# One fused VectorE operation for the second conditioning row of the modulation sums

## The chip, the cores and the metric

The kernel runs on one core of a Trainium2 chip. The metric is the device time of one execution in microseconds. The engines are named as in the profile: PE (TensorE, the matmuls), DVE (VectorE), ACT (ScalarE), POOL (GpSimd) and SP (SyncE, which here only issues DMAs). Each engine works through its own list of instructions in order; an instruction that waits holds up everything behind it on its engine.

## The reference, cut to what matters

The program is one block of a diffusion-style model followed by two transformer layers with experts. The change lies in the first block. Its modulation vectors are a matrix product of two conditioning rows, `c` for the 256 tokens of `x` and `c_ctx` for the 256 tokens of `ctx`, and its first feed-forward runs over all 512 tokens:

```python
mod   = (silu(c)     @ w_ada + b_ada)      # 9 * 1024 values, for x
mod_c = (silu(c_ctx) @ w_ada + b_ada)      # the same for ctx
h  = rmsnorm(x, g0) * (1 + mod[1]) + mod[0]
x  = x + 0.5 * mod[2] * rmsnorm((silu(h @ w_gate) * (h @ w_up)) @ w_out, g)
# ctx likewise with mod_c[0..2]; then both are modulated with entries 3 and 4
```

Entries 0 and 1 are needed before the feed-forward starts. Entries 2 to 4 are needed for both rows, entries 5 to 8 for `x` alone, and none of them before the feed-forward's end.

## The kernel before, in words

Entries 0 and 1 (2,048 of the 9,216 columns of `w_ada`) are computed by matmuls. The other 7,168 are cut into 56 tiles of 128 features. A tile of `w_mod` has its 128 features on the partitions and the 1,024 inputs along the row, so one value of `mod` is the sum along a row of weight times silu of a conditioning row. `crow[0]` and `crow[1]` hold these two rows, repeated on all partitions (their buffers show as `xn` in the profile, as does the scratch output `mscr`). `mod_tiles(n)` handles the next n tiles. Tiles 16 to 39 in its counting need both rows (`rs = 2`), tiles 40 to 71 one. For row 0 a DVE `scalar_tensor_tensor` (L600) multiplies and sums in one instruction, with a short accumulator read behind it. For row 1 POOL multiplies in place (L597) and ACT copies the product in place with a sum along the row (L598). When eight tiles are done, POOL adds the bias (L603).

These tiles are handled between the matmuls of the feed-forward. Its 22 hidden units of 128 features, j = 0 to 21, each take two weight tiles (gate and up), each 24 matmuls of 128x512: every fp32 product is taken as three products of a high and a low part (L154, L155, L156). `Weights._prepare` makes these parts from a loaded tile `raw`: ACT writes the high part (L100, `split..h`), DVE subtracts (L101, `split..l`). Only a few pairs of parts are kept ahead. After a unit's matmuls, ACT takes the silu (L502, `gate`), DVE multiplies (L504, `hid`), and the product is split again (ACT L150, DVE L151). After unit 10 the first half of the output product follows (`swiglu_out`), with tiles of `w_mod` between its steps, then units 11 to 21 and the second half.

The first 18 tiles of `w_mod` come through a ring of four buffers of their own (`own`), the rest through the six buffers of the weights' ring. All loads are issued by SP in one list (L83), each as soon as the last reader of its buffer is done. The order on each engine is set by the framework's scheduler when the kernel is built, not by the order of the code.

Of the kernel before, what the change touches and what calls it, by code (L numbers as in the profile page):

```python
# [13 lines left out]
AF = mybir.ActivationFunctionType  # L14
OP = mybir.AluOpType
# [109 lines left out]
def build(tc, A, out):  # L125
    nc = tc.nc
    es = ExitStack()
    V, SC, PE, GP = nc.vector, nc.scalar, nc.tensor, nc.gpsimd
# [29 lines left out]
    def rsqrt(pool, v, n):  # L158
        t = pool.tile([128, n], I32, name="rs_t", bufs=2)
        y = pool.tile([128, n], FT, name="rs_y", bufs=4)  # L160
        w = pool.tile([128, n], FT, name="rs_w", bufs=2)
        V.tensor_scalar(t, v.bitcast(I32), 1, None, op0=OP.logical_shift_right)
        V.tensor_scalar(y.bitcast(I32), t, -1.0, float(0x5F3759DF), op0=OP.mult, op1=OP.add)
        for _ in range(3):
            V.scalar_tensor_tensor(w, y, -0.5, v, op0=OP.mult, op1=OP.mult)
            V.tensor_tensor(out=w, in0=w, in1=y, op=OP.mult)
            V.scalar_tensor_tensor(y, w, 1.5, y, op0=OP.add, op1=OP.mult)  # L167
        return y
# [408 lines left out]
    crow, mscr = {}, None  # L577
# [4 lines left out]
    mscr = pf.tile([128, D], FT, name="xn", bufs=4)  # L582
# [5 lines left out]
    def mod_tiles(n):  # L588
        for _ in range(n):
            f = next(late)  # L590
            rs = 2 if f < 40 else 1
            src = own if f < 34 else st
            w = src.take(held)
            for r in range(rs):
                m = mod[:, f, r:r + 1]
                if r:
                    GP.tensor_tensor(out=w, in0=w, in1=crow[r], op=OP.mult)  # L597
                    SC.activation(w, w, AF.Copy, accum_out=m)  # L598
                else:
                    V.scalar_tensor_tensor(mscr, w, 1.0, crow[r], op0=OP.mult, op1=OP.mult, accum_out=m)  # L600
            if f % 8 == 7:
                m = mod[:, f - 7:f + 1, 0:rs]
                GP.tensor_tensor(out=m, in0=m, in1=cols[:, OB + f - 7:OB + f + 1, None].to_broadcast([128, 8, rs]), op=OP.add)  # L603
            src.more(held)

    st.slots("split", pf, 1, "in8", tag="hid2", bufs=12)
    for j in range(2, FT_N):
        hs.append(swiglu_in(pf, hT, 512, 12))
        mod_tiles(mod_in(j))
        if j == 10:  # L610
            Y = [pf.tile([128, D], FT, name="y1", tag="Y", bufs=4) for _ in range(4)]
            for h, t, P in swiglu_out(hs, range(4), after=lambda u: mod_tiles(mod_out(u))):
                (copy_act if t % 2 else V.tensor_copy)(Y[t][:, 512 * h:512 * h + 512], P)
            hs = []
            st.slots("split", pf, 1, "in19", tag="hid2", bufs=12)
# [11 lines left out]
    for r in range(2):  # L627
        ts = range(2 * r, 2 * r + 2)
        G = gate_rows(pf, 0, r, 0.5)
        posts = {t: Post(pf, tok[t], G, Y[t]) for t in ts}  # L630
        for h, t, P in swiglu_out(hs, ts, after=first_rows if r else (lambda u: mod_tiles(mod_last(u)))):
            posts[t].half(h, P)
        late_posts = [posts[t] for t in ts]
        if r:
            for p in late_posts:
                p.finish()
# [303 lines left out]
    for i in range(2):  # L940
        a, w = attention(i), within(i)
# [216 lines left out]
    for l in range(2):  # L1158
# [50 lines left out]
        r = rsqrt(pa, css.rearrange("p a b -> p (a b)"), 4)  # L1209
# [96 lines left out]
        for i in range(2):  # L1306
# [5 lines left out]
            for g0 in range(4):  # L1312
# [17 lines left out]
                for j in range(n // 2):  # L1330
# [3 lines left out]
                                           op0=OP.mult, op1=OP.add)  # L1334
# [14 lines left out]
            r = rsqrt(pa, ss, 4)  # L1349
# [38 lines left out]
        for p in range(2):  # L1388
            for i in range(2):
                for b in blocks(i):  # L1390
                    for s in range(2):
# [14 lines left out]
                        in1=rt[64:96, 1, None, :256].to_broadcast([32, 4, 256]), op=OP.add)  # L1406
# [107 lines left out]
        for d in range(DT):  # L1514
# [18 lines left out]
            m = pg.tile([128, 256], FT, name="msum", bufs=2)  # L1533
# [496 lines left out]
```

## Time and profile before

| | |
|---|---|
| median of three runs | 2044.76 us (2040.51 to 2051.39) |
| profiled execution, its own time | 2043.18 us |
| span in the profile | 2041.4 us |
| mean granted TensorE clock | 0.960 |
| PE busy | 1832.6 us (90%) |
| DVE busy | 1085.5 us (53%) |
| ACT busy | 785.5 us (38%) |
| POOL busy | 238.6 us (12%) |

The time outside the span is 1.8 us. Busy times are sums over the whole span, and an instruction that is held up after it has started counts as busy. The granted clock is 1 at 2.4 GHz and 0.5 at 1.2 GHz. The feed-forward's units with both rows and the first half of its output product lie between 60 and 215 us of the span.

### The profile page before, as it was taken

The numbers are of one execution on the slowest core, as the hardware profiler recorded it, in microseconds if no ns is written. First come the engines' busy times: TensorE is split into PE (matmuls) and PEld (weight loads), VectorE is DVE, ScalarE is ACT, GpSimd is POOL, SyncE is SP. The second block draws the span as 40 slices with busy tenths as digits, with TensorE's granted clock in tenths as the row PEclk, the third lists the DMA queues.
The fourth block names the chain that finished last, engine by engine and source line by source line (L and its number), as shares of the span: only waits on it lengthen the run. The fifth ranks groups of instructions, "written<-read, shape, count | busy, mean of one in ns | idle before, by whom it ended". The sixth has DMA issues, their size and how long they took to land. (4 is left out here: it accounts for less than half of the span.)

```text
span 2041.4 us, 29593 instructions
## 1 busy us (share of the span) xinstructions
PE 1832.6 (90%) x11486; PEld 1415.3 (69%) x11486; DVE 1085.5 (53%) x2086; ACT 785.5 (38%) x1369; POOL 238.6 (12%) x170
## 2 busy tenths in 40 slices
PE   6979999999989997999998998877879999979686
PEld 2768788877777797998888997424238889853331
DVE  4774465484646667555678556311257864641113
ACT  4443232353534445444455543211135465331111
POOL 2552100031122211000100011000010000200000
PEclk9989999999999998999998999998989899989798
DMA  8533475343131154555433478998963336899897
GB/s 322 190 141 122 170 254 208 132 155 106 65 117 63 63 169 135 188 188 190 148 125 103 135 268 311 360 412 345 413 263 135 105 124 204 309 357 413 352 413 282
DMA packets 120120, 436.63 MB, mean 214 GB/s; under 512 B 13616, under 2 KB 13664, under 8 KB 119968
## 3 DMA queue, kind: packets, MB, share of 16 engines
q1 hardware_dynamic: 116208, 422.63, 56.4%
q0 software_dynamic: 2608, 8.32, 1.2%
q10 hardware_dynamic: 1152, 3.67, 0.5%
q8 instruction: 94, 1.54, 0.3%
q14 instruction: 58, 0.48, 0.1%
HBM read 433.51 MB, written 1.05 MB: 213 GB/s over the span
## 5 line engine op out<-in xcount | busy, mean ns | idle before, releaser
L101 DVE TENSOR_TENSOR split7l<-raw,split7h 128x1024 fp32r<-128x1024 f32 x98 | 123.9, 1264 | 113.2 <-ACT split7h L100 112.9
L1697 PE MATMUL ax<-raw,xg 128*32 128x512 f32 x1024 | 166.1, 596 | 7.0 <-DMA raw<-in_moe 7.0
L101 DVE TENSOR_TENSOR split6l<-raw,split6h 128x1024 fp32r<-128x1024 f32 x99 | 127.4, 1286 | 84.5 <-ACT split6h L100 82.9
L100 ACT ACTIVATE split7h<-raw 128x1024 fp32r<-128x1024 f32 x101 | 106.7, 1057 | 166.6 <-PE mm L156 63.3
L100 ACT ACTIVATE split6h<-raw 128x1024 fp32r<-128x1024 f32 x102 | 107.9, 1058 | 153.8 <-PE mm L155 46.8
L1697 PEld LDWEIGHTS ax<-raw,xg 128*32 128x32 f32 x1024 | 37.2, 109 | 107.2 <-issue 59.6
L1668 PE MATMUL ax<-OH,X 128*128 128x128 f32 x512 | 71.8, 301 | 38.0 <-DVE OH L1659 35.9
L1668 PEld LDWEIGHTS ax<-OH,X 128*128 128x128 f32 x512 | 67.6, 213 | 54.7 <-DVE OH L1659 36.8
L600 DVE SCALAR_TENSOR_TENSOR xn<-raw,xn 128x1024 f32<-128x1024 f32 x56 | 85.0, 1517 | 22.0 <-DMA raw<-in_w_mod 21.2
L1724 PE MATMUL ax<-raw,ehT 128*32 128x512 f32 x512 | 77.1, 607 | 16.6 <-ACT ehT L147 15.6
L597 POOL TENSOR_TENSOR raw<-raw,xn 128x1024 f32<-128x1024 f32 x24 | 72.5, 3034 | 76.6 <-DVE xn L600 73.0
L1731 DVE SCALAR_TENSOR_TENSOR yl<-ax,gsl,yh 128x512 fp32r<-128x512 f32 x32 | 24.0, 751 | 99.0 <-ACT yh L1730 94.6
L377 ACT ACTIVATE xg<-ax,cols 128x128 f32<-128x128 f32 x64 | 24.1, 458 | 94.4 <-PE ax L1668 68.6
L1705 ACT ACTIVATE ehs<-ax 128x256 f32<-128x256 f32 x16 | 6.2, 384 | 137.7 <-PE ax L1697 137.7
L1706 DVE TENSOR_TENSOR ehs<-ax,ehs 128x256 f32<-128x256 f32 x16 | 6.8, 425 | 97.7 <-ACT ehs L1705 97.7
L1724 PEld LDWEIGHTS ax<-raw,ehT 128*32 128x32 f32 x512 | 17.6, 109 | 59.1 <-issue 27.8
L154 PE MATMUL mm<-hThi,split6h 128*128 128x512 f32 x128 | 53.1, 415 | 5.5 <-ACT split6h L100 3.5
L156 PE MATMUL mm<-hThi,split6l 128*128 128x512 f32 x128 | 53.0, 414 | 4.8 <-DVE split6l L101 4.8
L156 PE MATMUL mm<-hxhi,split7l 128*128 128x256 f32 x192 | 54.8, 285 | 1.2 <-POOL split7l L101 1.2
L154 PE MATMUL mm<-hxhi,split6h 128*128 128x256 f32 x192 | 54.2, 282 | 1.7 <-ACT split6h L100 1.7
L154 PE MATMUL mm<-hxhi,split7h 128*128 128x256 f32 x192 | 55.2, 288 | 0.0
L155 PE MATMUL mm<-hxlo,split7h 128*128 128x256 f32 x192 | 54.9, 286 | 0.0
(882 smaller groups left out, 5674.0 us busy)
## 6 DMA issues: line engine op xcount, KB each, us to landing
raw<-in_moe SPq DMA_DIRECT2D x384, 512.0 KB, 10.1
raw<-in_f_in SPq DMA_DIRECT2D x88, 512.0 KB, 4.3
raw<-in_w_gate SPq DMA_DIRECT2D x64, 512.0 KB, 3.5
raw<-in_w_mod SPq DMA_DIRECT2D x56, 512.0 KB, 4.3
raw<-in_f_out SPq DMA_DIRECT2D x55, 512.0 KB, 4.2
raw<-in_w_out SPq DMA_DIRECT2D x24, 512.0 KB, 6.8
raw<-in_w_br SPq DMA_DIRECT2D x20, 512.0 KB, 4.3
raw<-in_w_ada SPq DMA_DIRECT2D x16, 512.0 KB, 9.7
```

The costliest lines, as they stand in the source:

```text
L100: nc.scalar.activation(hi, x, AF.Copy)
L101: (nc.gpsimd if self.seq[i][1] == "pool" else nc.vector).tensor_tensor(out=lo, in0=x, in1=hi, op=OP.subtract)
L154: PE.matmul(o, lhsT=lh, rhs=rh, start=first, stop=False)
L155: PE.matmul(o, lhsT=lh, rhs=rl, start=False, stop=False)
L156: PE.matmul(o, lhsT=ll, rhs=rh, start=False, stop=last)
L377: SC.activation(o, p, AF.Identity, bias=b, scale=g)
L597: GP.tensor_tensor(out=w, in0=w, in1=crow[r], op=OP.mult)
L600: V.scalar_tensor_tensor(mscr, w, 1.0, crow[r], op0=OP.mult, op1=OP.mult, accum_out=m)
L1668: PE.matmul(P[:, 128 * b:128 * b + 128], lhsT=X[:, i, 128 * d:128 * d + 128], rhs=OH[:, i, :], start=i == 0, stop=i == 1)
L1697: PE.matmul(P[32 * s:32 * s + 32, :], lhsT=xg[:, k, 32 * s:32 * s + 32], rhs=ws[s](kk), start=k == 0, stop=k == DT - 1, tile_position=(0, ...
L1724: PE.matmul(P[32 * s:32 * s + 32, :], lhsT=d_["hT"][:, k, 32 * s:32 * s + 32], rhs=ws[s](k), start=k == 0, stop=k == 1, tile_position=(0, ...
L1731: V.scalar_tensor_tensor(yl, P, d_["gsl"], yh, op0=OP.mult, op1=OP.subtract)
```

## The change

The branch on the row is gone: both rows take the DVE instruction, on the same weight tile with another `crow`.

```diff
@@ mod_tiles @@
             for r in range(rs):
                 m = mod[:, f, r:r + 1]
-                if r:
-                    GP.tensor_tensor(out=w, in0=w, in1=crow[r], op=OP.mult)
-                    SC.activation(w, w, AF.Copy, accum_out=m)
-                else:
-                    V.scalar_tensor_tensor(mscr, w, 1.0, crow[r], op0=OP.mult, op1=OP.mult, accum_out=m)
+                V.scalar_tensor_tensor(mscr, w, 1.0, crow[r], op0=OP.mult, op1=OP.mult, accum_out=m)
```

In numbers: 24 POOL instructions and 24 ACT instructions less, 24 DVE instructions more. The list of PE is the same row for row. On the other engines the scheduler places some instructions otherwise; the lines of the DVE instruction and of all below it move up by four (L600 is now L596).

On ACT, around units 3 and 4 of the feed-forward before the change (`split` rows make weight parts, L502 and L150 belong to the hidden unit, `raw0` to `raw3` in L598 are the four buffers of the ring for `w_mod`):

```order
L598 ACTIVATE raw2_712,mod_136<-raw2_712 128x1024
L502 ACTIVATE gate_702<-mm_640 128x512
L598 ACTIVATE raw3_717,mod_136<-raw3_717 128x1024
L598 ACTIVATE raw0_791,mod_136<-raw0_791 128x1024
L598 ACTIVATE raw1_796,mod_136<-raw1_796 128x1024
L100 ACTIVATE split6h_696<-raw0_508 128x1024
L150 ACTIVATE hid2_706<-hid_704 128x512
L100 ACTIVATE split16h_775<-raw2_584 128x1024
```

The same place on ACT with the change:

```order
L502 ACTIVATE gate_700<-mm_638 128x512
L100 ACTIVATE split6h_694<-raw0_508 128x1024
L150 ACTIVATE hid2_704<-hid_702 128x512
L100 ACTIVATE split16h_771<-raw2_584 128x1024
L100 ACTIVATE split7h_740<-raw1_514 128x1024
```

The high part `split6h` stood behind three sums of the second row; now it follows the silu of the unit directly.

On DVE, from the product `hid` of unit 4 to that of unit 5 before the change (`xn_543` is the first conditioning row):

```order
L504 TENSOR_TENSOR hid_783<-mm_750,gate_781 128x512
L600 SCALAR_TENSOR_TENSOR xn_546,mod_136<-raw3_1028,xn_543 128x1024
L151 TENSOR_TENSOR hid2_785<-hid_783,hid2_785 128x512
L600 SCALAR_TENSOR_TENSOR xn_546,mod_136<-raw0_1102,xn_543 128x1024
L600 SCALAR_TENSOR_TENSOR xn_546,mod_136<-raw1_1107,xn_543 128x1024
L101 TENSOR_TENSOR split6l_824<-raw3_590,split6h_823 128x1024
L504 TENSOR_TENSOR hid_862<-mm_829,gate_860 128x512
```

The same place on DVE with the change (`xn_540` is the second conditioning row):

```order
L504 TENSOR_TENSOR hid_779<-mm_746,gate_777 128x512
L596 SCALAR_TENSOR_TENSOR xn_546,mod_136<-raw2_863,xn_543 128x1024
L151 TENSOR_TENSOR hid2_781<-hid_779,hid2_781 128x512
L596 SCALAR_TENSOR_TENSOR xn_546,mod_136<-raw2_863,xn_540 128x1024
L596 SCALAR_TENSOR_TENSOR xn_546,mod_136<-raw3_868,xn_543 128x1024
L596 SCALAR_TENSOR_TENSOR xn_546,mod_136<-raw3_868,xn_540 128x1024
L101 TENSOR_TENSOR split6l_818<-raw3_590,split6h_817 128x1024
L596 SCALAR_TENSOR_TENSOR xn_546,mod_136<-raw0_941,xn_543 128x1024
L596 SCALAR_TENSOR_TENSOR xn_546,mod_136<-raw0_941,xn_540 128x1024
L596 SCALAR_TENSOR_TENSOR xn_546,mod_136<-raw1_945,xn_543 128x1024
L504 TENSOR_TENSOR hid_856<-mm_823,gate_854 128x512
```

Three sums stood between the two products before, seven stand there now. The 18 tiles of the small ring end before the product of unit 5 in the order before, and before that of unit 7 in the order with the change.

## Rows read from the trace of the kernel before

**Rows 1.** Busy time by engine in three stretches, with counts in brackets

```profile
core 0: us, PE busy (x) PEld busy (x) DVE busy (x) ACT busy (x) POOL busy (x), PEclk, DMA share, GB/s
...
89.00:145.00 56.00, 42.81 (x150) 32.52 (x149) 45.29 (x40) 27.24 (x43) 36.15 (x15) 0.85 0.44 152
145.00:205.00 60.00, 60.00 (x259) 48.34 (x258) 29.43 (x32) 17.88 (x26) 15.58 (x5) 1.00 0.36 122
205.00:215.00 10.00, 6.87 (x22) 4.92 (x21) 7.53 (x10) 4.20 (x6) 4.43 (x3) 0.83 0.70 249
```

**Rows 2.** Waits, 60 to 215 us: total us, times, longest us

```profile
ACT raw L598 <- POOL raw L597: 60.1, 22, 4.9
...
DVE xn L600 <- DMA raw<-in_w_mod: 13.9, 5, 3.4
...
PE mm L156 <- DVE split6l L101: 4.8, 2, 2.9
...
PE mm L154 <- ACT split6h L100: 3.5, 1, 3.5
PE mm L154 <- ACT split7h L100: 3.3, 2, 1.9
PE mm L156 <- DVE split7l L101: 3.0, 2, 2.5
...
PE mm L155 <- DVE split7l L101: 1.8, 1, 1.8
```

**Rows 3.** Timeline of PE: start us, us, instruction, idle before and releaser

```profile
106.97 0.50 PE L154 MATMUL mm<-hThi,split6h 128*128 128x512 f32 x1 [3.50 <-ACT split6h L100]
```

**Rows 4.** Timeline of ACT before that matmul, columns as in group 3

```profile
98.97 1.06 ACT L598 ACTIVATE raw<-raw 128x1024 f32<-128x1024 f32 x1 [4.71 <-POOL raw L597]
...
102.32 1.06 ACT L598 ACTIVATE raw<-raw 128x1024 f32<-128x1024 f32 x1 [2.20 <-POOL raw L597]
...
104.83 1.06 ACT L598 ACTIVATE raw<-raw 128x1024 f32<-128x1024 f32 x1 [1.35 <-POOL raw L597]
...
105.88 1.04 ACT L100 ACTIVATE split6h<-raw 128x1024 fp32r<-128x1024 f32 x1
```

**Rows 5.** Timeline of POOL, 75 to 85 us

```profile
77.79 6.73 POOL L597 TENSOR_TENSOR raw<-raw,xn 128x1024 f32<-128x1024 f32 x2 [2.96 <-DVE xn L600]
```

**Rows 6.** Timeline of DVE around that POOL work

```profile
75.30 1.21 DVE L101 TENSOR_TENSOR split16l<-raw,split16h 128x1024 fp32r<-128x1024 f32 x1
76.44 1.21 DVE L600 SCALAR_TENSOR_TENSOR xn<-raw,xn 128x1024 f32<-128x1024 f32 x1
...
77.69 1.23 DVE L600 SCALAR_TENSOR_TENSOR xn<-raw,xn 128x1024 f32<-128x1024 f32 x1
...
78.84 3.42 DVE L101 TENSOR_TENSOR split6l<-raw,split6h 128x1024 fp32r<-128x1024 f32 x1
```

**Rows 7.** Groups of DVE instructions, 60 to 140 us: count, busy us, mean ns

```profile
L600 DVE SCALAR_TENSOR_TENSOR xn<-raw,xn 128x1024 f32<-128x1024 f32 x18 | 34.2, 1901 | 0.2
L101 DVE TENSOR_TENSOR split6l<-raw,split6h 128x1024 fp32r<-128x1024 f32 x4 | 10.6, 2654 | 2.1 <-ACT split6h L100 2.1
L151 DVE TENSOR_TENSOR hid<-hid,hid 128x512 fp32r<-128x512 f32 x5 | 9.1, 1822 | 1.3 <-ACT hid L150 1.3
L101 DVE TENSOR_TENSOR split7l<-raw,split7h 128x1024 fp32r<-128x1024 f32 x3 | 5.8, 1942 | 3.8 <-ACT split7h L100 3.8
```

**Rows 8.** Groups of DVE instructions, 215 to 360 us

```profile
L600 DVE SCALAR_TENSOR_TENSOR xn<-raw,xn 128x1024 f32<-128x1024 f32 x29 | 35.5, 1223 | 9.0 <-DMA raw<-in_w_mod 8.6
...
L151 DVE TENSOR_TENSOR hid<-hid,hid 128x512 fp32r<-128x512 f32 x9 | 6.2, 690 | 3.5 <-ACT hid L150 3.5
```

**Rows 9.** The sums on DVE, 145 to 205 us

```profile
L600 DVE SCALAR_TENSOR_TENSOR xn<-raw,xn 128x1024 f32<-128x1024 f32 x7 | 12.9, 1839 | 12.7 <-DMA raw<-in_w_mod 12.6
```

**Rows 10.** Busy time by engine, 60 to 140 us and 215 to 360 us

```profile
60.00:140.00 80.00, 66.81 (x259) 52.09 (x258) 67.80 (x59) 35.14 (x57) 54.20 (x20) 0.91 0.49 171
...
215.00:360.00 145.00, 145.00 (x625) 117.14 (x624) 80.14 (x107) 40.16 (x48) 3.73 (x4) 1.00 0.60 208
```

## The prediction

> **What bounds the kernel now.** I read the busy time by stretches first, around the lines of the diff. The feed-forward is a stage of matmuls: from 145 to 205 us PE is busy 60.00 of 60 us at full clock and gets through 259 matmuls, 0.2317 us each [rows 1], and from 215 to 360 us again 145.00 of 145 [rows 10]. There are two holes. From 89 to 145 us PE does 150 matmuls, which at that pace need 34.7 us, so 21.3 us are lost; from 205 to 215 us it does 22, worth 5.1 us, and 4.9 us are lost [rows 1]. Of these 26.2 us, 13.2 and 3.1 us are idle time (56 less 42.81, 10 less 6.87), and the remaining 9.9 us are matmuls at the lower level, 1.2 GHz: the granted clock in the two holes is 0.85 and 0.83 [rows 1]. So each idle microsecond was followed by another 0.6 us of loss through the clock.
>
> The second view is the list of waits. All of PE's waits from 60 to 215 us, 16.4 us in eight, are for weight parts, `split` tiles from ACT or DVE [rows 2]. The third view, the timeline, shows what is late. The matmul at 106.97 us idled 3.50 us for `split6h` [rows 3]. On ACT this split ran at 105.88 us, right behind three sums of the second row (L598), which had waited 4.71, 2.20 and 1.35 us for POOL's product [rows 4]. In the whole stretch ACT waits 60.1 us for POOL, in 22 pieces [rows 2]: the weight parts stand in a queue behind sums that PE does not wait for anywhere in the stretch.
>
> DVE is held up by the same POOL instructions in a way that the list of waits does not show. At 77.69 us a `scalar_tensor_tensor` takes 1.23 us; POOL begins two products at 77.79 us that last 6.73 us; the DVE subtraction that starts at 78.84 us then takes 3.42 us, against 1.21 us for the same shape at 75.30 us [rows 5, 6]. From 215 to 360 us, with POOL busy 3.73 us [rows 10], the 29 sums take 1223 ns on the mean and the shorter subtraction (L151) 690 [rows 8]; from 60 to 140 us the sums take 1901 ns, the long subtractions 2654 and 1942, the shorter ones 1822 [rows 7]. The blocked time inside DVE's "busy" is therefore 18 x 0.678 + 4 x 1.444 + 3 x 0.732 + 5 x 1.132 = 12.2 + 5.8 + 2.2 + 5.7 = 25.9 us in that stretch alone.
>
> **The change, part by part.** Removed: 24 POOL products, 3.4 us each where two take 6.73 [rows 5], and 24 ACT sums, 1.06 us each and some 0.1 us for the accumulator [rows 4]. Neither engine bounds the stage; what goes is ACT's 60.1 us of waiting ahead of splits [rows 2] and DVE's blocked time. POOL keeps only the bias additions here.
>
> Added: 24 DVE sums. One stands beside the next at 76.44 and 77.69 us, so it takes 1.25 us from start to start; a subtraction takes 1.14 us, from 75.30 to 76.44 [rows 6]. From 60 to 140 us, where 18 of the tiles lie, DVE pays 18 x 1.25 = 22.5 us and gets back 25.9 us: its total falls by about 3 us although it gets all the work. The other six fall in the output product, where DVE is busy 29.43 of 60 us [rows 1], and there they are covered.
>
> Moved: by the order on DVE, seven sums, a subtraction and the two short instructions lie between the products of units 4 and 5 (`hid_779` to `hid_856`). That is 7 x 1.25 + 1.14 + 2 x 0.69 = 11.3 us, while PE's unit of 48 matmuls lasts 48 x 0.2317 = 11.1 us. Between units 3 and 6 the other gaps hold five or six sums and two or three subtractions, and come to about the same. So over some five units, 2 to 6, DVE has no slack: a late weight tile or a late sum there reaches PE, unless a part that is already split covers it. After unit 7 the sums thin out and the slack is back. SP issues the loads of `w_mod` behind the release of their buffers, which now comes from DVE's second sum instead of ACT's.
>
> What a full DVE costs no row shows, so it is bounded. Below, nothing: the splits run a tile ahead of PE. Above, each of the five units ends one sum late, 5 x 1.25 = 6.3 us of idle, with the clock's 0.6 on top 10.0 us. I take half, 5.0 us. A second term is DVE's waits for loads of `w_mod`, now ahead of splits: of the 13.9 us in five waits, the longest 3.4 us [rows 2], nearly all lie between 145 and 205 us [rows 9], where PE is at 60.00 of 60 [rows 1], so before they cost nothing. I take one of the longest, half covered: 1.7 us, 2.7 us with the clock. On ACT the split's high part now waits only for the unit's own product behind which it stands (L150), which is inside the first term.
>
> Sum on the profiled execution: 2043.2 - 26.2 + 5.0 + 2.7 = 2024.7, so **2025 us**. This execution lies 1.6 us under the median of the three runs, which is small beside the terms. Nothing behind should take the gain back: from 215 to 360 us PE is busy 145.00 of 145 us [rows 10], every load waits for a buffer that the work ahead releases, and so the rest moves forward as a whole.
>
> **The rivals.** *DVE becomes the pace.* If the five units each end one sum late (10.0 us) and half of the 13.9 us of load waits reach PE with the clock's share (11.1 us), 21.1 of the 26.2 us are lost again: 2043.2 - 5.1 = 2038 us. For it speaks the order's 11.3 us against 11.1; against it, that DVE's total falls, and that a delay there does not hold up the next unit once the sums end.
>
> *DVE is overfilled, and the kernel is slower.* If the long DVE instructions are not POOL's doing but the load of the stage itself, nothing comes back: DVE is busy 67.80 of 80 us from 60 to 140 us [rows 10], with 22.5 us more it needs 90.3 us, and PE, which waits for its splits, gets there 10.3 us later: 2053.5 us. It decides where less than 10.3 us of the blocked time come back; above that the stretch fits into its 80 us. The Trainium skill's page "Perfetto Trace Analysis", section "Optimizing Scalar/DVE Operations", is on this side: where VectorE is saturated it advises to move work to ScalarE or even GpSimd, though it adds that between GpSimd and VectorE this may not help because they share a port. By its first half the change goes the wrong way, by its second the work never really left DVE. The trace agrees with the second half: 3.42 us beside POOL's product, 1.21 us just before it.
>
> *The change does little.* The holes may be filled by other late parts that the sums of row two now only hide, such as the loads in SP's list, or a stage behind may take the gain back. Against it, no PE wait in the stretch is for a load [rows 2]. Price: the whole 26.2 us stays, 2043 us.
>
> **How the numbers follow.** Chances: the forecast 0.73, DVE as the pace 0.16, overfilled 0.05, little 0.06. Half a per cent, 10.2 us, is about what a measurement of this kernel can tell from no change. The forecast is faster by more than that; of the second case about a fifth is, since its two terms are upper halves; the third is just beyond it on the other side. So faster 0.76 (0.73 and 0.03), same 0.19 (0.13 and 0.06), slower 0.05. The range: at best the full 26.2 us go, 2017, and the fastest of the three runs lies 2.7 us under the profiled one, so 2014. The upper end takes in DVE as the pace, 2038, and a little run-to-run spread: 2040. What is left out above is overfilled and little, some 0.11.
>
> **What would show it.** After: no L597 and L598; the 80 sums at about 1.22 us in every stretch, none near 3.4 us; the subtractions from 60 to 140 us near 1.22 us as well; POOL's busy time down by about 70 us (54.20 of them stand between 60 and 140 us, with three quarters of the tiles), ACT's by about 28 (24 x 1.16), DVE's within 6 us of before, since 24 sums at 1.22 us, 29 us, stand against 25.9 us of blocked time in the first hole and some more in the second. The hole from 89 to 145 us shrinks to one or two waits of 1 to 2 us, behind rows of sums on DVE or a sum that waits for `w_mod`; the one at 205 us goes. From 60 us to the first copy of the output product (L613, then L609) the program is some 20 us shorter, and as much at the end. The prediction is wrong if the DVE instructions stay long without POOL, if PE's idle time in the stretch stays over 10 us, or if the stretch shrinks and the end does not.

## The result, and the profile after

The changed kernel takes 2021.37 us in the median of six runs (2018.24 to 2022.66), the kernel before 2042.62 us beside it (six runs, 2037.43 to 2051.39). The ratio is 0.989, with a 95% interval of 0.9873 to 0.9906, so the change makes the kernel faster by 21 us. The profiled execution took 2022.66 us, its span is 2020.9 us and its mean granted clock 0.960.

The first part of the profile after gives each engine's busy time, share and instructions:

```profile
PE 1833.8 (91%) x11486; PEld 1418.2 (70%) x11486; DVE 1079.6 (53%) x2134; ACT 760.1 (38%) x1321; POOL 167.0 (8%) x146
```

DVE has 24 sums more and is 5.9 us less busy than before (1085.5). POOL loses 71.6 us and ACT 25.4 us, as much as 24 sums of 1.06 us.

The busy time by stretches after, with the columns of [rows 1] (PE, PEld, DVE, ACT, POOL, granted clock, DMA share, GB/s):

```profile
89.00:145.00 56.00, 56.00 (x243) 45.29 (x243) 45.82 (x71) 14.93 (x19) 2.51 (x2) 1.00 0.52 172
145.00:205.00 60.00, 60.00 (x258) 48.27 (x257) 36.43 (x50) 15.59 (x18) 1.25 (x1) 1.00 0.51 177
205.00:215.00 10.00, 10.00 (x45) 8.02 (x44) 1.90 (x2) 2.12 (x2) 0.00 (x0) 1.00 0.33 107
60.00:140.00 80.00, 80.00 (x347) 64.81 (x346) 71.91 (x108) 22.95 (x30) 2.51 (x2) 1.00 0.61 202
```

Both holes of [rows 1] are gone: PE is busy without a gap at full clock and does 243 matmuls from 89 to 145 us, where it did 150. From 60 to 140 us DVE is busy 71.91 us, against 67.80 in [rows 10], but that is for 108 instructions instead of 59: PE is 88 matmuls further in these 80 us, and DVE's work for nearly two more units is in them.

The list of waits from 60 to 215 us has no row of PE any more. DVE's wait for loads stands as in [rows 2], and POOL's long waits cost nothing:

```profile
POOL mod L599 <- DVE xn L596: 123.0, 3, 60.0
...
DVE xn L596 <- DMA raw<-in_w_mod: 12.5, 5, 3.5
```

The groups of DVE instructions from 60 to 140 us after (count, busy us, mean ns, idle before), which answer to [rows 7]:

```profile
L596 DVE SCALAR_TENSOR_TENSOR xn<-raw,xn 128x1024 f32<-128x1024 f32 x38 | 46.4, 1221 | 4.2 <-DMA raw<-in_w_mod 3.5
L101 DVE TENSOR_TENSOR split6l<-raw,split6h 128x1024 fp32r<-128x1024 f32 x5 | 6.1, 1225 | 2.0 <-ACT split6h L100 1.9
L101 DVE TENSOR_TENSOR split7l<-raw,split7h 128x1024 fp32r<-128x1024 f32 x5 | 6.1, 1223 | 0.5 <-ACT split7h L100 0.5
...
L151 DVE TENSOR_TENSOR hid<-hid,hid 128x512 fp32r<-128x512 f32 x8 | 5.5, 684 | 0.0
```

The same instruction shapes that took 1901, 2654, 1942 and 1822 ns beside POOL's products now take 1221, 1225, 1223 and 684.

The timeline of DVE after, around the unit with seven sums, and at its longest wait for a load (start us, us, instruction, idle before):

```profile
101.53 0.69 DVE L504 TENSOR_TENSOR hid<-mm,gate 128x512 f32<-128x512 f32 x1
...
107.80 1.23 DVE L101 TENSOR_TENSOR split6l<-raw,split6h 128x1024 fp32r<-128x1024 f32 x1 [0.16 <-ACT split6h L100]
...
112.62 0.69 DVE L504 TENSOR_TENSOR hid<-mm,gate 128x512 f32<-128x512 f32 x1
...
134.78 1.22 DVE L596 SCALAR_TENSOR_TENSOR xn<-raw,xn 128x1024 f32<-128x1024 f32 x1 [3.47 <-DMA raw<-in_w_mod]
```

From one product `hid` to the next DVE takes 11.09 us, which is PE's unit of 11.1 us. DVE has next to no slack here (the one idle time that the rows list is 0.16 us), as forecast, and yet PE waits for nothing.

How much the stretch gave is read at the first copy of the output product. The line L613 before (durations in ns, then first and last start in us):

```profile
L613 DVE COPY y<-mm x4: 683/689/692, 223.1 to 255.4; 128x512 f32<-128x512 f32 x4
```

and its line after, L609:

```profile
L609 DVE COPY y<-mm x4: 683/687/691, 197.1 to 229.4; 128x512 f32<-128x512 f32 x4
```

It starts 26.0 us earlier. The spans differ by 20.5 us. So nearly all of the 26.2 us that I had counted in the two holes came back in the stretch, and some 5.5 us are not there at the end of this pair of profiles; the experiments come to that.

### The profile page after: what moved, and what is told of

Its sections match the earlier page's. It is cut to its first block, busy times and chain, and to the rows that moved or that the text cites. A ratio compares the mean times of both kernels' runs of the same rounds, so it can differ in the third digit from the quotient of the medians.

```text
span 2020.9 us, 29550 instructions
## 1 busy us (share of the span) xinstructions
PE 1833.8 (91%) x11486; PEld 1418.2 (70%) x11486; DVE 1079.6 (53%) x2134; ACT 760.1 (38%) x1321; POOL 167.0 (8%) x146
## 5 line engine op out<-in xcount | busy, mean ns | idle before, releaser
L101 DVE TENSOR_TENSOR split6l<-raw,split6h 128x1024 fp32r<-128x1024 f32 x99 | 122.0, 1232 | 85.7 <-ACT split6h L100 85.4
L596 DVE SCALAR_TENSOR_TENSOR xn<-raw,xn 128x1024 f32<-128x1024 f32 x80 | 97.7, 1222 | 21.4 <-DMA raw<-in_w_mod 19.9
L377 ACT ACTIVATE xg<-ax,cols 128x128 f32<-128x128 f32 x64 | 24.1, 458 | 94.4 <-PE ax L1664 94.4
L155 PE MATMUL mm<-hxlo,split6h 128*128 128x256 f32 x192 | 54.5, 284 | 0.0
L156 PE MATMUL mm<-hxhi,split6l 128*128 128x256 f32 x192 | 54.1, 282 | 0.0
L1726 ACT ACTIVATE yh<-ax,gsl 128x512 fp32r<-128x512 f32 x32 | 22.0, 687 | 83.3 <-PE ax L1720 72.3
```

Source lines behind the costliest of these rows:

```text
L101: (nc.gpsimd if self.seq[i][1] == "pool" else nc.vector).tensor_tensor(out=lo, in0=x, in1=hi, op=OP.subtract)
L155: PE.matmul(o, lhsT=lh, rhs=rl, start=False, stop=False)
L156: PE.matmul(o, lhsT=ll, rhs=rh, start=False, stop=last)
L377: SC.activation(o, p, AF.Identity, bias=b, scale=g)
L1726: SC.activation(yh, P, AF.Copy, scale=d_["gsl"])
```

## The experiments

They ran in three groups, each beside runs of the kernel before on the same chip. The question was not whether the change helps but by which of the two causes in the prediction: the queue on ACT, where splits stand behind sums that wait for POOL, or DVE held up by POOL's product. A further question was why a full DVE costs nothing.

**The changed kernel once more** (`again`, unchanged).

> The changed kernel unchanged, a second time. Theory: the change empties both holes (26.2 us), and 8 us of what stands ahead at 1200 us are lost again in the two layers behind, to 3.4 or 6.8 us at the lower clock that depend on how the time falls and not on the work. Then the second profile shows no PE wait from 60 to 215 us again, but the half-clock pieces near 1190 and 1720 us may be elsewhere or missing, and the time is 2015 to 2024 us. Rival: the loss belongs to the changed kernel (other order, other load times); then both pieces stand at the same matmuls again and the time is within 2 us of 2021.

Measured: 2022.24 us (four runs, 2017.87 to 2024.42) beside 2042.62; ratio 0.9885 (0.9857 to 0.9914). The first copy of `y` starts at 197.5 us, where it was at 197.1. The result repeats. So do the pieces at the lower clock behind: the mean granted clock is 0.97 from 1162 to 1212 us (0.93 in the first profile) and 0.89 from 1710 to 1740 us (0.89 from 1705 to 1735 us in the first). This run therefore does not tell the theory from its rival; the second profile of the kernel before does, which has such a piece too.

**POOL's product put back, for nobody** (`pool_back`). The changed kernel, with POOL multiplying each two-row tile again into a spare buffer that nothing reads. ACT has no sums, and DVE's list of instructions is that of the changed kernel, row for row.

```diff
                 V.scalar_tensor_tensor(mscr, w, 1.0, crow[r], op0=OP.mult, op1=OP.mult, accum_out=m)
+                if r:
+                    GP.tensor_tensor(out=pscr, in0=w, in1=crow[r], op=OP.mult)
```

> The changed kernel with the POOL product of the old form added back behind each second sum, into a spare buffer that nobody reads; the list of DVE stays the same row for row, ACT has no sums of the second row. Theory (POOL's product blocks DVE, and DVE has no slack from unit 2 to unit 6): the sums and subtractions beside it take up to 3.4 us again, 18 tiles lose some 2 us each on a DVE that is full, about 36 us, of which PE loses 20 to 35 with the clock: 2040 to 2060 us, slower than the kernel before or equal to it. Rival (DVE has slack, the queue on ACT alone made the holes): PE waits under 3 us from 60 to 215 us and 2019 to 2025 us.

Measured: 2056.6 us (2051.6 to 2063.43) beside 2042.62; ratio 1.007 (1.0044 to 1.0097). With the same DVE list it is slower than the kernel before. Its busy time by stretches (columns as above) shows the hole again and a second one behind it:

```profile
89.00:145.00 56.00, 43.44 (x166) 33.71 (x164) 55.48 (x56) 9.91 (x14) 32.23 (x12) 0.88 0.49 159
145.00:205.00 60.00, 54.38 (x221) 43.20 (x222) 45.05 (x51) 15.41 (x20) 15.29 (x6) 0.94 0.38 123
```

and its DVE groups from 60 to 140 us the stretched instructions:

```profile
L597 DVE SCALAR_TENSOR_TENSOR xn<-raw,xn 128x1024 f32<-128x1024 f32 x26 | 45.9, 1765 | 0.5
L151 DVE TENSOR_TENSOR hid<-hid,hid 128x512 fp32r<-128x512 f32 x5 | 12.2, 2438 | 0.0
```

DVE is "busy" 55.48 of 56 us with 56 instructions; the changed kernel does 71 in 45.82. POOL's product also keeps each tile's buffer longer, but a DVE that is busy for all but 0.5 us has no late load in this stretch. PE's longest wait from 60 to 215 us is 5.6 us for a subtraction on DVE, in its list of waits:

```profile
PE mm L156 <- DVE split6l L101: 12.9, 3, 5.6
PE mm L156 <- DVE split7l L101: 4.9, 1, 4.9
```

**POOL busy, but reading nothing** (`pool_write`). The same, with a memset of the spare buffer instead of the product (`GP.memset(pscr, 0.0)`).

> The changed kernel with a POOL memset of the same 128x1024 buffer behind each second sum, which only writes; the list of DVE is the same. Theory (what blocks is POOL's reading beside a DVE instruction with two inputs in SBUF): sums stay at 1.22 us, no PE wait, 2018 to 2024 us. Rival (any POOL instruction of that size blocks DVE): sums and subtractions beside a memset take 2 us or more, and the time goes to 2030 us or above.

Measured: 2020.51 us (2017.87 to 2023.81) beside 2042.62; ratio 0.9886 (0.9858 to 0.9914), the whole gain. The memsets wait for nothing and so run early, 20.26 us of them between 60 and 89 us. The POOL group from 60 to 215 us:

```profile
L599 POOL MEMSET pscr<- 128x1024 f32 x22 | 21.1, 957 | 1.3
```

and the sums on DVE from 60 to 140 us. From 60 to 81 us POOL is busy 19.79 of 21 us with memsets, and DVE's sums and long subtractions there take 1.22 to 1.23 us each, as everywhere else:

```profile
L597 DVE SCALAR_TENSOR_TENSOR xn<-raw,xn 128x1024 f32<-128x1024 f32 x38 | 46.4, 1221 | 4.5 <-DMA raw<-in_w_mod 3.8
```

So it is not enough that POOL works: the product, which reads two tiles, holds DVE up, and the memset, which reads none, does not. A POOL instruction that reads one whole tile was not run.

**ACT's sums out, first attempt** (`no_act`). The kernel before, with a one-column copy on POOL in place of ACT's sum.

```diff
                     GP.tensor_tensor(out=w, in0=w, in1=crow[r], op=OP.mult)
-                    SC.activation(w, w, AF.Copy, accum_out=m)
+                    GP.tensor_copy(m, w[:, 0:1])
```

> The kernel before without the ACT sums of the second row (POOL multiplies as before, and then copies one column into mod, so these values of mod are not the sums). ACT no longer waits for POOL ahead of splits, DVE is still blocked by POOL. Theory (the queue on ACT makes most of the idle time, since DVE is at 68 of 80 us even with the blocked time): the holes shrink from 26 us to 3 to 10, 2022 to 2030 us. Rival (the blocked DVE makes the holes): PE still loses 15 us or more there, 2033 to 2043 us.

Measured: 2046.67 us (ten runs, 2038.2 to 2053.88) beside 2042.62; ratio 1.0009 (0.999 to 1.0027). My theory that ACT's queue makes most of the idle time fell: the queue is gone and nothing was gained. But the experiment was not clean, as POOL's copies are not small; its POOL groups from 60 to 215 us:

```profile
L597 POOL TENSOR_TENSOR raw<-raw,xn 128x1024 f32<-128x1024 f32 x24 | 70.4, 2932 | 53.0 <-DVE xn L600 46.5 <-issue 6.4
L598 POOL COPY mod<-raw 128x1 f32<-128x1 f32 x24 | 21.0, 875 | 1.5
```

A copy of one column takes 875 ns, 21.0 us in all. So it was done again without anything in their place.

**The kernel before, profiled once more** (`before_again`), to see how far two profiles of it differ.

> The kernel before, a second profile, because the first may be a lucky one: in it no half-clock piece stands at the merge behind the first layer's attention (1210 to 1230 us), while the other four profiles have one there. Theory (the later pieces fall as they fall): the loss in the two holes is again 24 to 28 us, and a piece of 3.4 or 6.8 us may stand near 1215 us this time. Rival (the changed kernel brings these pieces about): again none there. Time 2037 to 2050 us.

Measured: 2046.05 us, one run. PE's waits in the stretch are 14.2 us in all, where they were 16.4 [rows 2], again for splits of ACT and DVE. From 60 to 215 us it does 574 matmuls, 133.0 us of work at 0.2317 us each, so 22.0 us are lost, less than the 24 to 28 expected. Its first copy of `y` starts at 219.4 us:

```profile
L613 DVE COPY y<-mm x4: 682/689/692, 219.4 to 251.7; 128x512 f32<-128x512 f32 x4
```

That is 3.7 us earlier than in the first profile, so the stretch's gain is 22.3 to 26.0 us, by which profile of before one takes.

**Only the blocked DVE** (`blocked_only`). The kernel before without ACT's sums of row two and with nothing in their place; those values of `mod` are set to zero at the start.

```diff
+    V.memset(mod[:, 16:40, 1:2], 0.0)
...
                     GP.tensor_tensor(out=w, in0=w, in1=crow[r], op=OP.mult)
-                    SC.activation(w, w, AF.Copy, accum_out=m)
```

> The kernel before without the ACT sums of the second row and without anything in their place (these values of mod are set to zero at the start): POOL's product still blocks DVE, ACT's queue is free of it. In the run with a copy on POOL in its place nothing was gained, but that copy made POOL 21 us busier. Theory now (the blocked DVE alone makes the holes): PE loses 15 to 28 us from 60 to 215 us, all its waits for DVE's subtractions, 2034 to 2046 us. Rival (the extra copy did it, the queue on ACT is the cause): under 10 us lost, 2020 to 2029 us.

Measured: 2045.85 us (ten runs, 2040.26 to 2049.11) beside 2042.55; ratio 1.0013 (0.9997 to 1.0029). No gain, with no queue on ACT. The first hole stands nearly as in [rows 1], where PE was busy 42.81 us and did 150 matmuls. From 60 to 215 us PE does 565 matmuls, which leaves 24.1 us lost, between the two profiles of before (554 and 574 matmuls, 26.6 and 22.0 us):

```profile
89.00:145.00 56.00, 43.84 (x166) 34.06 (x165) 51.04 (x42) 11.13 (x15) 39.81 (x14) 0.88 0.49 165
```

But without ACT's sums DVE is held up longer: from 60 to 140 us it is busy 76.56 us with 62 instructions, where [rows 10] have 67.80 us with 59:

```profile
60.00:140.00 80.00, 67.83 (x270) 53.51 (x270) 76.56 (x62) 17.82 (x24) 58.47 (x20) 0.91 0.49 172
```

PE's waits from 60 to 215 us are 16.4 us as before, now all for DVE (total us, times, longest us):

```profile
PE mm L156 <- DVE split6l L101: 7.0, 2, 5.6
PE mm L156 <- DVE split7l L101: 5.1, 2, 5.0
PE mm L155 <- DVE split7l L101: 4.3, 1, 4.3
```

How the two engines hold each other up is seen on its timelines. POOL runs three products in a row:

```profile
112.10 9.97 POOL L598 TENSOR_TENSOR raw<-raw,xn 128x1024 f32<-128x1024 f32 x3 [2.96 <-DVE xn L600]
```

In these 10 us DVE gets through three instructions, each as long as a product, and the next one is short again:

```profile
113.27 3.29 DVE L600 SCALAR_TENSOR_TENSOR xn<-raw,xn 128x1024 f32<-128x1024 f32 x1
...
116.49 3.35 DVE L101 TENSOR_TENSOR split7l<-raw,split7h 128x1024 fp32r<-128x1024 f32 x1
119.76 3.39 DVE L600 SCALAR_TENSOR_TENSOR xn<-raw,xn 128x1024 f32<-128x1024 f32 x1
...
123.19 1.22 DVE L600 SCALAR_TENSOR_TENSOR xn<-raw,xn 128x1024 f32<-128x1024 f32 x1
```

One instruction of each per 3.3 us: one product costs DVE about 2.1 us (3.3 less 1.22), the sum and the subtraction alike. That is nearly the whole product: the shortest of the 24 in the kernel before takes 2.35 us.

**Only the queue** (`queue_only`). The kernel before with three memsets of the tile in place of POOL's product: ACT's sums still wait for POOL, but POOL reads nothing. The sums are of zeros.

```diff
-                    GP.tensor_tensor(out=w, in0=w, in1=crow[r], op=OP.mult)
+                    for _ in range(3):
+                        GP.memset(w, 0.0)
                     SC.activation(w, w, AF.Copy, accum_out=m)
```

> The kernel before with POOL's product replaced by three memsets of the same tile, which only write and so don't block DVE, but last about as long (3 x 0.96 us); ACT sums the tile as before, behind POOL (the sums are of zeros). Theory (blocked DVE is the cause): sums and subtractions on DVE near 1.22 us, PE loses 0 to 6 us from 60 to 215 us, 2018 to 2027 us, though ACT waits for POOL 30 us or more. Rival (the queue on ACT is enough by itself): PE waits for the high parts from ACT again and loses 12 us or more, 2030 to 2043 us.

Measured: 2020.83 us (2019.36 to 2025.14) beside 2042.55; ratio 0.9899 (0.9869 to 0.9929). The whole gain is there, with all of ACT's sums still in its queue. Its busy time by stretches has POOL nearly as busy as [rows 1] (36.15 us) and PE without a gap:

```profile
89.00:145.00 56.00, 56.00 (x243) 45.34 (x242) 29.46 (x41) 26.46 (x41) 30.99 (x35) 1.00 0.47 168
```

and its list of waits has ACT still waiting for POOL, half as long as in [rows 2], and no row of PE:

```profile
ACT raw L599 <- POOL raw L598: 30.8, 17, 3.9
```

The sums on DVE from 60 to 140 us, with POOL busy 53.19 of these 80 us, are short:

```profile
L601 DVE SCALAR_TENSOR_TENSOR xn<-raw,xn 128x1024 f32<-128x1024 f32 x19 | 23.2, 1223 | 14.9 <-DMA raw<-in_w_mod 14.7
```

**A longer queue** (`queue_long`). The same with four memsets, to bring ACT's waiting up to that of before.

> As the run with three memsets in place of POOL's product, but with four (3.8 us a tile, more than the product's 3.4), because ACT's wait there was 30.8 us, half of the 60 us in the kernel before; the sums on ACT are of zeros again. Theory (the queue on ACT does not reach PE, the blocked DVE does): ACT waits for POOL 45 to 70 us, PE loses 0 to 4 us from 60 to 215 us, 2018 to 2026 us. Rival (the queue counts from that length on): PE waits for the high parts from ACT and 8 us or more are lost, 2028 us or above.

Measured: 2024.63 us (2019.31 to 2029.41) beside 2044.74; ratio 0.9919 (0.9888 to 0.9951). The waits from 60 to 215 us:

```profile
ACT raw L599 <- POOL raw L598: 35.0, 16, 4.7
...
PE mm L156 <- DVE split6l L101: 0.5, 1, 0.5
PE mm L154 <- ACT split6h L100: 0.5, 1, 0.5
```

ACT's waiting came to 35.0 us only, less than the 45 to 70 expected; the 60.1 us of before were not reached. Up to this length the queue gives PE 0.5 us of waiting for ACT in the profiled execution. That execution is the fastest of the four (2019.31 us); two of the others took 2028.71 and 2029.41 us, in the range of the rival, and no profile shows where.

**A third sum** (`third`). The changed kernel with one more DVE sum for each two-row tile, the same one again: 24 x 1.25 = 30 us of DVE on top.

```diff
                 V.scalar_tensor_tensor(mscr, w, 1.0, crow[r], op0=OP.mult, op1=OP.mult, accum_out=m)
+                if r:
+                    V.scalar_tensor_tensor(mscr, w, 1.0, crow[r], op0=OP.mult, op1=OP.mult, accum_out=m)
```

> The changed kernel with a third sum on DVE for each two-row tile (the second one twice): 24 x 1.25 = 30 us more on DVE, and by its order six or seven sums in each unit from 2 to 10 instead of 2 to 6. Theory (DVE was full at 11.1 to 11.3 us a unit and PE never waited, so a unit that stays at that pace costs nothing, however long it goes on): PE loses 0 to 5 us, 2018 to 2027 us. Rival (DVE had no slack left; what is added lands on PE): 30 us and the clock's share, 2045 us or more.

Measured: 2017.78 us (2014.84 to 2020.39) beside 2042.55; ratio 0.988 (0.985 to 0.9909). From 89 to 205 us DVE is busy 110.3 of 116 us (82.3 in the changed kernel), and PE still has no gap:

```profile
89.00:145.00 56.00, 56.00 (x243) 45.34 (x242) 54.69 (x86) 15.04 (x19) 1.25 (x1) 1.00 0.54 176
145.00:205.00 60.00, 60.00 (x258) 48.22 (x258) 55.59 (x84) 15.75 (x18) 1.85 (x2) 1.00 0.55 187
```

**Less split ahead** (`less_ahead`). In the changed kernel most subtractions end 8 to 9 us before PE first uses their part: one of `split6l` ends at 109.03 us and is used at 118.24. I took this lead for what covers the full DVE. The experiment takes one pair of parts out of the supply by leaving out one line:

```diff
-    st.slots("split", pf, 1, "in8", tag="hid2", bufs=12)
     for j in range(2, FT_N):
```

> The changed kernel without the third buffer pair for split weights in units 2 to 8, so that only two pairs are in turn there as in the later units. Theory (the full DVE cost nothing because the parts are ready 8 to 9 us ahead of PE there, and only 3 to 4 us ahead with two pairs): with up to five sums in a row ahead of a subtraction, 6.3 us, PE now waits, 3 to 12 us with the clock: 2023 to 2033 us. Rival (the scheduler's order keeps the parts in time without that lead): no PE wait, 2017 to 2024 us.

Measured: 2022.84 us (2019.93 to 2022.97) beside 2044.74; ratio 0.9898 (0.9875 to 0.9922). The lead fell to 2.8 to 3.8 us, and PE has no wait:

```profile
89.00:145.00 56.00, 56.00 (x241) 45.05 (x241) 46.06 (x70) 16.13 (x20) 1.35 (x2) 1.00 0.51 169
```

The theory fell: a lead of 3 us is enough here. But the run changed more than the lead. On its DVE list the subtractions from 80 to 125 us stand behind three or four sums each, about one every 5.5 us (85.88, 91.30, 96.94, 102.49, 108.14 us), where in the changed kernel up to seven sums stand between two subtractions. Whether the order of the changed kernel would do with so short a lead is not shown.

**Only the first 18 tiles** (`own_only`). The tiles of the small ring have both sums on DVE; the six later ones keep POOL and ACT.

```diff
-                if r:
+                if r and f >= 34:
                     GP.tensor_tensor(out=w, in0=w, in1=crow[r], op=OP.mult)
```

> One part alone: the 18 tiles of the small ring take the DVE sum for both rows, the six tiles between the steps of the output product keep POOL's product and ACT's sum (3.4 us each on POOL). Theory: the first hole goes (21 us in the first profile), the second, near 205 us in the kernel before, stays at 3 to 5 us: 2022 to 2029 us. Rival (the second hole is an echo of the first, from loads that come late): it goes too, 2018 to 2022 us.

Measured: 2023.2 us (2021.51 to 2027.65) beside 2044.74; ratio 0.9912 (0.9886 to 0.9938). From 89 to 145 us PE is busy 56.00 of 56 us; a small second hole stays, with two waits of PE. Its busy time by stretches and its waits:

```profile
145.00:205.00 60.00, 56.75 (x231) 44.98 (x230) 34.53 (x39) 19.36 (x27) 17.59 (x6) 0.94 0.48 167
```

```profile
PE mm L155 <- DVE split7l L101: 1.8, 1, 1.8
PE mm L154 <- ACT split7h L100: 1.5, 1, 1.5
```

Six tiles left on POOL and ACT make the second hole, and the 18 taken away made the first. In the stretch the second is worth some 5.3 us, since the first copy of the output product comes that much later than in the changed kernel (202.4 against 197.1 us); the intervals of the two ratios overlap, so the times do not show it.

## Why the prediction was right, and where its steps were off

**The time.** 2025 us was forecast and 2021.4 measured, inside the range of 2014 to 2040. The sum's main term, the 26.2 us of the two holes, was right: the stretch shrank by 26.0 us against the profile of before from which the sum was made, and by 22.3 against its second profile.

**The cause.** The prediction gave two, and only one is shown to make the holes. POOL's product lengthens DVE's instructions, and that is enough by itself: put back for nobody it costs more than the whole gain (`pool_back`), without ACT's sums the holes stay (`blocked_only`), and with POOL's reads gone they close although ACT still waits 30.8 us for POOL (`queue_only`). The other cause, that weight parts stand on ACT behind sums that wait for POOL, is not needed: with the sums taken out, PE's waits came to the same 16.4 us, all of them for DVE, where 9.6 us of them were before [rows 2].

The equal sums do not show that the queue did nothing in the kernel before, since DVE was held up more without ACT's sums. Its trace shows both cases. The prediction read the queue from the wait of 3.50 us at 106.97 us [rows 3, 4]. There it hid behind DVE: DVE stood idle only 0.32 us for the high part, was then held up by a product, and PE waited again for what it wrote. An earlier high part would have brought PE on by about 0.3 us there, an estimate from these rows:

```profile
106.95 2.61 DVE L101 TENSOR_TENSOR split6l<-raw,split6h 128x1024 fp32r<-128x1024 f32 x1 [0.32 <-ACT split6h L100]
```

```profile
109.62 0.79 PE L156 MATMUL mm<-hThi,split6l 128*128 128x512 f32 x1 [1.91 <-DVE split6l L101]
```

At 91 us it did reach PE. DVE itself stood idle for a high part that was on ACT behind a sum that had waited 3.47 us for POOL:

```profile
91.30 1.23 DVE L101 TENSOR_TENSOR split7l<-raw,split7h 128x1024 fp32r<-128x1024 f32 x1 [3.82 <-ACT split7h L100]
```

```profile
91.32 0.50 PE L154 MATMUL mm<-hThi,split7h 128*128 128x512 f32 x1 [1.92 <-ACT split7h L100]
```

PE waited 0.54 us more for the low part, 2.46 us in all; in `blocked_only` the same matmuls wait 0.15 us. So the queue had a small share in the kernel before, some 2.3 us of PE's 16.4 at this place. What stays open is how much a queue of the full 60.1 us would cost without blocked DVE instructions; 35.0 us cost 1.0 us of waiting in the one profile.

The Trainium skill's page "SBUF — State Buffer", section "Who interferes with whom", states this rule: a DVE instruction with two inputs in SBUF contends with a GpSimd instruction that reads SBUF, and not with one that only writes it. This case agrees on both halves: sums take 3.29 and 3.39 us beside products (`blocked_only`), and 1221 ns on the mean with memsets of the same size running beside a part of the sums (`pool_write`).

**The cost of the sums.** 22.5 us added and 25.9 us given back was the forecast for DVE from 60 to 140 us. The whole program shows DVE 5.9 us less busy, within the 6 us given. POOL's 71.6 us and ACT's 25.4 answer to the 70 and 28 that were forecast.

**The terms that were mis-sized.** "What a full DVE costs" was put at 5.0 us and the wait for a load at 2.7 us; both measure 0, and the one or two waits of PE that were to remain did not appear. DVE runs at PE's pace in that unit as forecast (11.09 us), and with a third sum it is busy 54.69 of 56 us, but PE never waits. The 3.47 us wait for a load of `w_mod` at 134.78 us reaches no matmul. With both at 0 the sum is 2017.0 us, 4.4 us under the median. That the forecast came within 3.6 us is therefore in part luck: 7.7 us of cost that was not there stood in for 4.4 us that the sum did not have. Why a full DVE costs nothing is open. My first reason, the long lead of the split parts, was not borne out by `less_ahead`, but there the sums also stood between the subtractions in shorter rows.

**Nothing behind takes the gain back.** By the matmul's number in PE's list, which is the same list, the first pair of profiles differs by 26.0 us at the end of the first output product, 25.6 us around 1714 us, 22.5 around 1812 and 20.1 at the end. Part of what is lost lies in the stage behind each layer's attention, where PE has short pieces at the lower clock in one execution and not in another. The busy time there, before in its first profile:

```profile
1190.00:1240.00 50.00, 48.05 (x404) 47.23 (x403) 33.07 (x45) 23.13 (x33) 12.46 (x8) 1.00 0.77 275
```

before in its second profile:

```profile
1188.00:1238.00 50.00, 48.42 (x381) 47.60 (x380) 31.88 (x44) 21.70 (x31) 12.48 (x8) 0.93 0.72 263
```

and after:

```profile
1162.00:1212.00 50.00, 49.22 (x390) 48.62 (x389) 31.62 (x43) 20.97 (x31) 12.46 (x8) 0.93 0.75 271
```

At a mean of 0.93, 3.5 us of work are missing in 50 us. The kernel before shows this too in its second profile, so the change is not needed for it; its first profile happened to have none. Against that second profile the output product comes 22.3 us earlier and the span is 23.4 us shorter, so nothing is lost behind. In `third` the lead over the first profile is 25.9 us at the output product and still 25.7 at the end. So the gain in the program is that of the stretch, 22 to 26 us, less what such pieces take in a given execution; the medians, 21 us apart, lie just under it. Why these pieces come and go is not settled here.

**The rivals.** DVE did run level with PE, so the case of 2038 us named the right place, but no unit ended late. The overfilled DVE (2053.5 us) needed less than 10.3 us of blocked time to come back, and all of it came back. Its time is nearly that of `pool_back` (2056.6 us), which is what it looks like when all sums are on DVE and the blocking stays. That the change does little (2043 us) is excluded by the interval.

## What to carry to other kernels

Compare the mean duration of one instruction shape in stretches with and without GpSimd's work beside it: VectorE's blocked time counts as busy and stands in no list of waits. An operation that was moved to GpSimd to relieve VectorE can cost VectorE more (here about 2.1 us a product) than doing it there (1.25 us). When a wait has two possible causes, take each away by itself: the row of a wait names who came last, and with the named queue gone here the same time was waited for another engine. And look whether taking one cause away made the other larger, as it did here.

## What the hardware showed that was not expected

A DVE instruction with one input in PSUM was not lengthened: the product L504 (`hid` from `mm` and `gate`) took 678 to 692 ns in all six of its instances from 60 to 140 us before, two of which, at 86.80 and 136.00 us, ran wholly beside POOL's products, while the subtraction L151 of the same size with both inputs in SBUF took 1822 on the mean [rows 7]. What a whole product costs a DVE instruction with two inputs in SBUF did not depend on that instruction's length: in `blocked_only` four of the L151 take 2.86 to 2.89 us, where one beside no product takes 0.68, which is 2.2 us more; the sums and the long subtraction shown above take 2.1 to 2.2 us more than 1.22. And a copy of one column on POOL took 875 ns, almost as long as a memset of 128x1024 (957 ns).
